# Gate loads, squares and weight sums at other points of the program, and another order at the start of the up stage and at its last pair

## The chip, the cores and the metric

The kernel runs on one NeuronCore of one Trainium2 chip. The metric is the device time of one execution in microseconds; lower is better. A core has a matrix engine (TensorE, PE in the profile, with its weight loads as PEld), three engines for elementwise work (VectorE = DVE, ScalarE = ACT, GpSimd = POOL) and SyncE (SP), which here issues most of the DMAs. The engines run their own instruction streams in order and wait for each other by semaphores.

## The reference

One layer of a hybrid encoder on a prompt of 1024 tokens and a batch of 8 x 16 sample tokens (1152 columns in the kernel). Cut to what matters here:

```python
z = rms_norm(x, g_mix) @ w_in              # latents, retention q/k/v, gates ga and gb
attn = latent_attention(z)                 # 8 heads
ret  = retention(z)                        # 4 heads, chunkwise, gated
a_d = attn @ w_o_branch[:1024]
r_d = ret  @ w_o_branch[1024:]
merged = sigmoid(ga) * a_d + sigmoid(gb) * r_d
x = x + merged @ w_out
u = rms_norm(x, g_ffn) @ w_ffn_up          # 1024 -> 2 * 2816
c = causal_conv_width_3(u) + b
x = x + (silu(c[gate]) * c[value]) @ w_ffn_down
```

The outputs are x of prompt and sample, the new latents and rope keys, the retention states and the last two rows of u.

## The kernel before

Tokens lie along the free axis (T = 1152 columns, three chunks of CH = 384), features on the 128 partitions. Every f32 factor is split into two parts, hi (a cast on ScalarE, L228) and lo (a difference on VectorE, L229), and a product is made of three matmuls, hi*hi, lo*hi and hi*lo. So before a weight tile (`wraw` loaded by SP, `whi`, `wlo`) or an activation tile can be used, ScalarE and then VectorE must have handled it.

The stages that the change touches, in order of time:

- *Gate stage* (to about 165 us). Tiles 0 to 13 of the gate weights; `gate_out` applies the sigmoid and stores the tile to `s_gate`. Between the tiles stand loads and sums for later: the up stage multiplies with sums of quarters of the up weights. `sum_load(j)` (L352, L353) has SP load the quarters `prg` and `prv`, `sum_store(j)` has POOL add them (L344 to L347, `psum`) and store them to `s_w`. Beside it runs `norm`: column sums of squares on TensorE (L339), `ss`, the power on POOL (L284, `inv`), `ivsq` (L450) and a diagonal matrix `diag` (L330) with which TensorE spreads the row over the partitions (L333). The last two sums stand in the kv stage behind it (L525).
- *Branch layers* (about 1340 to 1662 us). Three layers of 8 output tiles: `w_or` on the retention rows (`ret_out`, L1293: `xf` = product * gate), `w_oa` on the attention rows (`att_out`, L1300 and L1301: `xf` += product * gate) and `w_out` on `xf` (`res_out`). The gate tile `mg` has two buffers and is loaded by POOL's own queue. After each output tile `presum_half` lets POOL add half of a weight sum. In the third layer `mg` holds x, `res_row` adds the product (L1312), scales into `y` (L1313) and stores the sum to `s_x` (L1314); `squares` then squares `mg` in place (L1319) and adds it to `acc` (L1320).
- *Start of the up stage* (about 1662 to 1700 us). The up product splits the rows in a two-level scheme with seven blocks (b11, t1, t2, t3, t4, b21, b22), each of four row tiles k = 0 to 3. The blocks that have no place while the third layer runs are stored to memory by `combine` and come back in `reload` (tile `z`, two buffers; L1363). `last_row` handles the last output tile of the third layer, with ScalarE and VectorE held to the written order. `fourth` and `fifth` follow in `then`, which is called after each of the seven products of a pair.
- *Last pair and start of the down stage* (about 2160 to 2200 us). The convolution taps and the activation of the last pair, splits of the first down weights (`down_w`) and of the stored activations `ar`, reloaded through POOL's queue (L1565), in groups.

A scheduler places the instructions of each engine from the program order and its own costs, except inside `in_order`, where the named engines keep the written order. What stands where is read below from the instruction lists of the two built kernels.

## Time and profile before

| | us |
|---|---|
| median of 3 runs | 2457.23 (2455.23 to 2459.61) |
| the profiled execution, whole | 2458.73 |
| its span in the trace | 2456.9 |
| PE busy | 2392.1 (97%) |
| DVE busy | 1420.9 (58%) |
| ACT busy | 946.4 (39%) |
| POOL busy | 476.5 (19%) |
| mean granted clock of TensorE, of 1 | 0.983 |

The span runs from the first to the last instruction in the trace; the profiled execution took 1.83 us more. TensorE is busy nearly throughout, so time shows in two things: where it idles, and where its clock is low. In the rows of a timeline stand the start, the busy time of a run of equal instructions, engine, line, operation, output and inputs, the count, and in brackets the idle time before it with the instruction that ended it. In the waits stand the total, the count and the longest.

### The profile page before, as it was taken

How to read it: one execution, taken by the hardware profiler on the slowest of the kernel's cores; microseconds unless marked ns; L12 is line 12 of the kernel's file. 1: busy time of each engine (PE TensorE's matmuls, PEld its weight loads, DVE VectorE, ACT ScalarE, POOL GpSimd, SP SyncE). 2: the span in 40 equal slices, each digit the busy share in tenths (PEclk: the TensorE clock that was granted, in tenths of full speed). 3: DMA queues.
4: the chain of work that ended last, by engine and by line, in shares of the span. 5: the costliest groups of instructions: out<-in, count | busy, mean ns of one | idle time of the engine just before them, and what ended most of it. 6: DMA issues, size and time to landing. Idle time of an engine off the chain costs nothing.

```text
span 2456.9 us, 38559 instructions
## 1 busy us (share of the span) xinstructions
PE 2392.1 (97%) x14888; PEld 2284.6 (93%) x14888; DVE 1420.9 (58%) x2858; ACT 946.4 (39%) x2210; POOL 476.5 (19%) x727
## 2 busy tenths in 40 slices
PE   9999999999999989999999989998999999999999
PEld 8999998998999968787998989997999999999999
DVE  7233456456249857444887333557888888884442
ACT  5221333333236635664665120334333333353331
POOL 2721000000003302332110324141111111121100
PEclk9999999999999999998999989998999999999999
DMA  6952311210225576525674565373333333377652
GB/s 238 383 188 96 114 56 35 69 64 23 76 78 170 159 249 206 168 85 147 206 210 136 195 210 182 132 257 119 104 120 111 108 100 120 111 239 233 213 162 92
DMA packets 175991, 366.29 MB, mean 149 GB/s; under 512 B 15296, under 2 KB 92224, under 8 KB 174016
## 3 DMA queue, kind: packets, MB, share of 16 engines
q1 hardware_dynamic: 81728, 213.00, 26.4%
q0 software_dynamic: 35824, 88.52, 11.7%
q10 hardware_dynamic: 58256, 62.30, 7.4%
q8 instruction: 117, 1.92, 0.3%
q14 instruction: 66, 0.54, 0.1%
HBM read 252.65 MB, written 111.13 MB: 148 GB/s over the span
## 4 chain that ended last, share of the span: by engine, by line
PE 78%; DMA 6%; issue 5%; DVE 5%; POOL 4%; ACT 2%; SPq 0%; ACTq 0%; POOLq 0%; DVEq 0%
PE mm L188 48%; PE mm L1422 19%; PE sm L188 4%; DMA pr<-w_up 3%; PE sc L188 3%; PE apo L188 2%; PE apt L1140 1%; POOL psum L344 1%; DVE wlo L229 1%; POOL psum L346 1%; DMA mg<-s_gate 1%; DMA s_x<-mg 1%; POOL psum L345 1%; DMA s<-s_ret 1%; POOL psum L347 1%
## 5 line engine op out<-in xcount | busy, mean ns | idle before, releaser
L228 ACT CAST whi<-wraw 128x1024 fp32r<-128x1024 f32 (+3 forms) x223 | 221.0, 999 | 518.5 <-PE mm L188 312.3
L229 DVE TENSOR_TENSOR wlo<-wraw,whi 128x1024 fp32r<-128x1024 f32 (+3 forms) x223 | 259.1, 1168 | 199.9 <-ACT whi L228 198.6
L1422 PE MATMUL mm<-xt,whi 128*128 128x288 f32 x1408 | 284.7, 297 | 6.8 <-DVE u L1475 5.2
L1422 PEld LDWEIGHTS mm<-xt,whi 128*128 128x128 f32 x1408 | 228.4, 190 | 7.4 <-DVE u L1475 5.4
L188 PE MATMUL mm<-whi,xh 128*128 128x256 f32 (+2 forms) x720 | 228.2, 333 | 0.7 <-DVE gsig L410 0.7
L188 PE MATMUL mm<-whi,xl 128*128 128x256 f32 (+2 forms) x720 | 225.3, 329 | 0.0
L188 PE MATMUL mm<-wlo,xh 128*128 128x256 f32 (+2 forms) x720 | 224.8, 329 | 0.3 <-DVE wlo L229 0.3
L1422 PE MATMUL mm<-xb,whi 128*128 128x288 f32 x1056 | 213.0, 296 | 2.1 <-ACT r L1480 1.2
L1422 PE MATMUL mm<-xt,wlo 128*128 128x288 f32 x704 | 209.2, 297 | 0.0
L1422 PEld LDWEIGHTS mm<-xb,whi 128*128 128x128 f32 x1056 | 170.5, 189 | 2.9 <-ACT r L1480 1.4
L1422 PE MATMUL mm<-xb,wlo 128*128 128x288 f32 x528 | 156.6, 297 | 1.3 <-DVE wlo L229 1.3
L188 PE MATMUL mm<-rh,whi 128*128 128x384 f32 x576 | 135.3, 342 | 14.3 <-DVE xf L1293 8.9
L188 PEld LDWEIGHTS mm<-whi,xl 128*128 128x128 f32 x720 | 132.5, 190 | 12.1
L188 PEld LDWEIGHTS mm<-whi,xh 128*128 128x128 f32 x720 | 132.6, 190 | 10.6 <-issue 0.7
L188 PEld LDWEIGHTS mm<-wlo,xh 128*128 128x128 f32 x720 | 132.6, 190 | 9.8 <-DVE wlo L229 0.5
L188 PE MATMUL mm<-act,whi 128*128 128x384 f32 x528 | 134.3, 335 | 3.4 <-ACT whi L228 3.4
L188 PE MATMUL mm<-rl,whi 128*128 128x384 f32 x576 | 134.2, 340 | 3.4 <-DVE rl L229 3.3
L188 PE MATMUL mm<-act,dwhi 128*128 128x384 f32 x528 | 134.5, 335 | 0.0
L1422 PEld LDWEIGHTS mm<-xt,wlo 128*128 128x128 f32 x704 | 133.6, 190 | 0.0
L188 PE MATMUL mm<-rh,wlo 128*128 128x384 f32 x576 | 133.1, 338 | 0.0
L188 PE MATMUL mm<-xh,whi 128*128 128x384 f32 x528 | 123.9, 340 | 2.9 <-ACT whi L228 2.1
L188 PE MATMUL mm<-xl,whi 128*128 128x384 f32 x528 | 122.1, 337 | 0.0
(495 smaller groups left out, 5690.9 us busy)
## 6 DMA issues: line engine op xcount, KB each, us to landing
wraw<-w_dn SPq DMA_DIRECT2D x48, 512.0 KB, 3.7
s_q<-uqT ACTq DMA_DIRECT2D x36, 384.0 KB, 3.3
s_w<-psum POOLq DMA_DIRECT2D x12, 1024.0 KB, 8.7
aq<-s_q POOLq DMA_DIRECT2D x8, 1536.0 KB, 9.0
ar<-s_act POOLq DMA_DIRECT2D x21, 576.0 KB, 5.8
wraw<-w_up SPq DMA_DIRECT2D x22, 512.0 KB, 3.7
wraw<-s_w SPq DMA_DIRECT2D x22, 512.0 KB, 4.3
wraw<-s_w SPq DMA_DIRECT2D x44, 256.0 KB, 3.0
```

What stands on the lines that cost most here:

```text
L188: E.matmul(out, l, r, start=start, stop=stop)
L228: A.copy(hi, src)
L229: return V.tensor_tensor(out=lo, in0=src, in1=hi.bitcast(F32), op=ALU.subtract)
L344: G.tensor_tensor(out=s[:, 1], in0=rg[:, 0], in1=rv[:, 0], op=ALU.add)
L345: G.tensor_tensor(out=s[:, 2], in0=rv[:, 0], in1=rv[:, 1], op=ALU.add)
L346: G.tensor_tensor(out=s[:, 0], in0=s[:, 2], in1=rg[:, 0], op=ALU.add)
L347: G.tensor_tensor(out=s[:, 3], in0=s[:, 0], in1=rg[:, 1], op=ALU.add)
L1140: E.transpose(pt[:, j * 256 + e * P:j * 256 + (e + 1) * P], pm[e][:, jj * P:(jj + 1) * P], ident)
L1422: E.matmul(banks[bank][c], l[:, ks], x, start=bool(first) and k + e == 0, stop=k + e == 5, skip_group_check=not first)
```

## The change

- The sums of the gate stage: the load of a sum and its adds come one tile later; the kv stage takes three sums instead of two.
- The branch layers: the loads of the gate tiles (and of x in the third layer) come from one list, two ahead, each next one called for after a tile is used; squares of a tile are called for at the start of the next tile; t1 is made in place in `y1`.
- The start of the up stage: `reload` has three buffers; the splits of the first two weights stand ahead of the first reloads; the third weight, the last block splits, the reloads and the squares of tile 7 move among the first three products (`rest`).
- The last pair: the splits of the last third of the first down weights stand ahead of the taps of the gate half and its activation.

```diff
@@ -456,9 +456,9 @@
                 stream.start(norm())
                 for f in range(2, 13):
                     gate_out(f, fm_tile(mm, wslot(d["w_gate"][f], D), xr))
-                    if f > 2:
-                        pend.append(sum_load(f - 3, wk, 2))
                     if f > 3:
+                        pend.append(sum_load(f - 4, wk, 2))
+                    if f > 4:
                         sum_store(*pend.pop(0), wk, 2)
                 sum_store(*pend.pop(0), wk, 2)
 
@@ -522,8 +522,8 @@
                         if k == 3:
                             stream.tick()
                     stream.start(kv_out(t, ps))
-                    if t in (2, 5):
-                        pend.append(sum_load(10 + t // 5, wk, 1))
+                    if t % 3 == 1:
+                        pend.append(sum_load(9 + t // 3, wk, 1))
                     elif pend:
                         sum_store(*pend.pop(), wk, 1)
                     stream.tick()
@@ -1227,13 +1227,14 @@
-        def new_rows(mm, w, f0, f1, fill):
+        def new_rows(mm, w, f0, f1, load):
+            ahead = [load(k) for k in range(2)] if load else []
             wts = [bslot(d[w][f]) for f in (f0, f1)]
             rows = []
 
             def row(k):
                 hi, lo = slot("rh", f"r{2 * k}"), slot("rl", f"r{2 * k + 1}")
-                fill(k, hi, lo)
+                split(hi, lo, (ahead.pop(0) if ahead else load(k)) if load else xf[k])
                 rows.append((hi, lo))
                 return hi, lo
 
@@ -1256,8 +1257,8 @@
                     S.dma_start(rv, quarters(d["w_up"][NJ + j])[:, :, hs])
                 pend.append((j, hs, rg, rv))
 
-        def layer(mm, w, order, fill, out):
-            rows, first = new_rows(mm, w, order[0], order[1], fill)
+        def layer(mm, w, order, load, out):
+            rows, first = new_rows(mm, w, order[0], order[1], load)
             for i, f in enumerate(order):
                 ps = fm_tile(mm, bslot(d[w][f]), rows) if i > 1 else first[i]
                 out(f, ps)
@@ -1284,28 +1285,39 @@
 
         xf = [None] * 8
 
+        sources = [s_gate[8 + f] for f in range(8)] + [s_gate[f] for f in range(8)] + [d["x_fm"][f] for f in (0, 4, 1, 5, 2, 6, 3, 7)]
+        loaded = []
+
+        def load_g():
+            if sources:
+                g = wk.tile([P, T], F32, name="mg", bufs=2)
+                G.dma_start(g, sources.pop(0))
+                loaded.append(g)
+
+        load_g()
+        load_g()
+
         def ret_out(f, ps):
             xf[f] = slot(f"xf{f}", f"e{f}", dt=F32)
-            g = wk.tile([P, T], F32, name="mg", bufs=2)
-            G.dma_start(g, s_gate[8 + f])
+            g = loaded.pop(0)
             for c in range(NCH):
                 cs = slice(c * CH, (c + 1) * CH)
                 V.tensor_tensor(out=xf[f][:, cs], in0=ps[c], in1=g[:, cs], op=ALU.mult)
+            load_g()
 
         def att_out(f, ps):
-            g = wk.tile([P, T], F32, name="mg", bufs=2)
-            G.dma_start(g, s_gate[f])
+            g = loaded.pop(0)
             for c in range(NCH):
                 cs = slice(c * CH, (c + 1) * CH)
                 V.tensor_tensor(out=g[:, cs], in0=ps[c], in1=g[:, cs], op=ALU.mult)
                 V.tensor_tensor(out=xf[f][:, cs], in0=xf[f][:, cs], in1=g[:, cs], op=ALU.add)
+            load_g()
 
         acc = fwt.tile([P, T], F32, name="acc")
         ys = {}
 
         def res_row(f, ps):
-            g = wk.tile([P, T], F32, name="mg", bufs=2)
-            G.dma_start(g, d["x_fm"][f])
+            g = loaded.pop(0)
             y = ys[f] = wk.tile([P, T], F32, name="y", bufs=2)
             for c in range(NCH):
                 cs = slice(c * CH, (c + 1) * CH)
@@ -1321,18 +1333,27 @@
             else:
                 A.activation(acc, g, AF.Square)
 
+        unsquared = []
+
+        def settle():
+
+            if unsquared:
+                squares(*unsquared.pop())
+                load_g()
+
         ha, hb = slice(0, HT), slice(HT, T)
         late_work = []
 
         def res_out(f, ps):
             if f == 7:
                 return last_row(ps)
+            settle()
             g, y = res_row(f, ps)
             if f < 4:
                 block("b11", f, y[:, ha])
             else:
                 combine(f - 4)
-            squares(g, f)
+            unsquared.append((g, f))
 
         def combine(k):
 
@@ -1344,9 +1365,9 @@
                 else:
                     S.dma_start(s_t[name, k], src)
 
-            t1 = wk.tile([P, HT], F32, name="t1")
+            t1 = y1[:, ha]
             t2 = wk.tile([P, HT], F32, name="t2")
-            V.tensor_tensor(out=t1, in0=y1[:, ha], in1=y1[:, hb], op=ALU.subtract)
+            V.tensor_tensor(out=t1, in0=t1, in1=y1[:, hb], op=ALU.subtract)
             V.tensor_tensor(out=t2, in0=y2[:, hb], in1=t1, op=ALU.add)
             done("t2", t2)
             done("b21", y2[:, ha])
@@ -1359,20 +1380,21 @@
 
         def reload(blocks):
             for b, k in blocks:
-                z = wk.tile([P, HT], F32, name="z", bufs=2)
+                z = wk.tile([P, HT], F32, name="z", bufs=3)
                 S.dma_start(z, s_t[b, k])
                 block(b, k, z)
 
         def last_row(ps):
 
             y1 = ys[3]
-            t1 = wk.tile([P, HT], F32, name="t1")
+            t1 = y1[:, ha]
             t2 = wk.tile([P, HT], F32, name="t2")
             with in_order(ET.Activation, ET.DVE):
-                reload(late[:4])
+                settle()
                 raw = up_raw(0)
                 w = [wtile(raw[i], D, i) for i in range(2)]
-                V.tensor_tensor(out=t1, in0=y1[:, ha], in1=y1[:, hb], op=ALU.subtract)
+                reload(late[:4])
+                V.tensor_tensor(out=t1, in0=t1, in1=y1[:, hb], op=ALU.subtract)
                 block("t1", 3, t1)
                 g, y2 = res_row(7, ps)
                 V.tensor_tensor(out=t2, in0=y2[:, hb], in1=t1, op=ALU.add)
@@ -1380,25 +1402,27 @@
                 block("b21", 3, y2[:, ha])
                 V.tensor_tensor(out=y1[:, hb], in0=y1[:, hb], in1=y2[:, hb], op=ALU.subtract)
                 block("t3", 3, y1[:, hb])
-                w.append(wtile(raw[2], D, 2))
-
-            def fourth():
-                V.tensor_tensor(out=y2[:, ha], in0=y2[:, ha], in1=t2, op=ALU.subtract)
-                block("t4", 3, y2[:, ha])
-                reload(late[4:7])
-
-            def fifth():
-                block("b22", 3, y2[:, hb])
-                squares(g, 7)
-                reload(late[7:10])
-
-            late_work.extend((raw, w, fourth, fifth))
+
+            def rest(n):
+                if n == 0:
+                    w.append(wtile(raw[2], D, 2))
+                    V.tensor_tensor(out=y2[:, ha], in0=y2[:, ha], in1=t2, op=ALU.subtract)
+                    block("t4", 3, y2[:, ha])
+                    reload(late[4:5])
+                elif n == 1:
+                    reload(late[5:7])
+                    block("b22", 3, y2[:, hb])
+                else:
+                    reload(late[7:10])
+                    squares(g, 7)
+
+            late_work.extend((raw, w, rest))
 
         order = list(range(8))
         raw_row = lambda src: (lambda t: (S.dma_start(t, src), t)[1])(wk.tile([P, T], F32, name="y", bufs=2))
-        layer(mm, "w_or", order, lambda k, hi, lo: split(hi, lo, raw_row(s_ret[k])), ret_out)
-        layer(mm, "w_oa", order, lambda k, hi, lo: split(hi, lo, raw_row(s_att[k])), att_out)
-        layer(mm, "w_out", [0, 4, 1, 5, 2, 6, 3, 7], lambda k, hi, lo: split(hi, lo, xf[k]), res_out)
+        layer(mm, "w_or", order, lambda k: raw_row(s_ret[k]), ret_out)
+        layer(mm, "w_oa", order, lambda k: raw_row(s_att[k]), att_out)
+        layer(mm, "w_out", [0, 4, 1, 5, 2, 6, 3, 7], None, res_out)
 
 
 
@@ -1577,8 +1601,7 @@
         AT = [(5, 6), (7, 8), (9, 10), (13, 14), (15, 16), (19, 20), (21, 22), (23, 24)]
         AT = [tuple(DS[i] for i in t) for t in AT]
 
-        raw_w, w, fourth, fifth = late_work
-        w.append(None)
+        raw_w, w, rest = late_work
         raw_n = up_raw(1)
         prev = None
         acts, wa, wb = [], [], []
@@ -1602,14 +1625,14 @@
                         prev.tap(v, prev.uv, prev.cv, 0)
                         prev.tap(g, prev.ug, prev.cg, 1)
                     else:
-                        fourth()
+                        rest(0)
                 elif n == 1:
                     me.read_u2(ps)
                     if prev:
                         prev.tap(g, prev.ug, prev.cg, 0)
                     else:
-                        fifth()
-                    w[3] = wtile(raw_w[3], 512, 3)
+                        rest(1)
+                    w[3:] = [wtile(raw_w[3], 512, 3)]
                     if prev:
                         A.activation(prev.cg, prev.cg, AF.Silu)
                     if last:
@@ -1617,6 +1640,7 @@
                         me.rw = [down_raw(0, 0), down_raw(1, 0)]
                 elif n == 2:
                     if not j:
+                        rest(2)
                         open_up()
                     me.read_c11(ps)
                     if prev:
@@ -1700,11 +1724,11 @@
                 prev.tap(v, prev.uv, prev.cv, 0)
                 group(4)
                 group(5)
+                wa += down_w(rw[4], 2, set_a)
+                wb += down_w(rw[5], 2, set_b)
                 prev.tap(j, prev.ug, prev.cg, 1)
                 prev.tap(j, prev.ug, prev.cg, 0)
                 A.activation(prev.cg, prev.cg, AF.Silu)
-                wa += down_w(rw[4], 2, set_a)
-                wb += down_w(rw[5], 2, set_b)
                 group(6)
                 prev.product()
                 acts += act_split(prev.cv[:, None, :CH], act_tiles(AT[7]))
```

POOL's list at the end of the first branch layer and the start of the second, before: `psum` and its store are a weight sum, `s_gate14` and `15` are the gates of the last two tiles of the first layer, `s_gate0` and `1` those of the second.

```order
L347 TENSOR_TENSOR psum_16064<-psum_16064,pr_15842 128x256
L1249 DMA s_w15_142<-psum_16064 512x1x256
L1290 DMA mg_15734<-s_gate14_95 128x1152
L1290 DMA mg_15831<-s_gate15_96 128x1152
L1297 DMA mg_16056<-s_gate0_81 128x1152
L1297 DMA mg_16074<-s_gate1_82 128x1152
L344 TENSOR_TENSOR psum_16082<-pr_16070,pr_16071 128x256
```

And after:

```order
L347 TENSOR_TENSOR psum_16068<-psum_16068,pr_15846 128x256
L1250 DMA s_w15_142<-psum_16068 512x1x256
L1294 DMA mg_15547<-s_gate14_95 128x1152
L1294 DMA mg_15644<-s_gate15_96 128x1152
L1294 DMA mg_15741<-s_gate0_81 128x1152
L1294 DMA mg_15838<-s_gate1_82 128x1152
L344 TENSOR_TENSOR psum_16086<-pr_16074,pr_16075 128x256
```

Lines have other numbers; no instruction has another place here. In all three layers one of the 24 loads, the fourth, stands one sum instruction earlier.

SP's list at the start of the up stage, before: `z` are block reloads, `s_t`, `s_b` the stored blocks, `wraw` the weights of the second pair and of the rest of it, `s_x` the stores of x.

```order
L1363 DMA z_17561<-s_t320_154 128x576
L1363 DMA z_17566<-s_t100_149 128x576
L1314 DMA s_x3_114<-mg_17463 128x1152
L1363 DMA z_17571<-s_t110_150 128x576
L1363 DMA z_17576<-s_t120_151 128x576
L1363 DMA z_17670<-s_t400_155 128x576
L1363 DMA z_17675<-s_t410_156 128x576
L1212 DMA wraw_17628<-w_up 128x1024
L1212 DMA wraw_17630<-s_w1_128 128x1024
L1314 DMA s_x7_118<-mg_17602 128x1152
L1212 DMA wraw_17632<-s_w1_128 128x512
L1212 DMA wraw_17632<-w_up 128x512
```

And after:

```order
L1384 DMA z_17576<-s_t320_154 128x576
L1384 DMA z_17581<-s_t100_149 128x576
L1384 DMA z_17586<-s_t110_150 128x576
L1326 DMA s_x3_114<-mg_17354 128x1152
L1212 DMA wraw_17620<-w_up 128x1024
L1212 DMA wraw_17622<-s_w1_128 128x1024
L1384 DMA z_17591<-s_t120_151 128x576
L1384 DMA z_17666<-s_t400_155 128x576
L1384 DMA z_17700<-s_t410_156 128x576
L1384 DMA z_17705<-s_t420_157 128x576
L1326 DMA s_x7_118<-mg_17462 128x1152
L1212 DMA wraw_17624<-s_w1_128 128x512
```

The third reload moved ahead of the store of x, and the two large weight loads moved ahead of the fourth reload. On ScalarE and VectorE the splits of the first two weights now stand ahead of the splits of the first four reloads; the difference t1 and everything up to the split of t3 stays behind those four; u (L1475) stands ahead of the second and third of the next three reloads; and acc of tile 7 (L1320) behind the last three.

ScalarE's list at the last pair, before: `ar` are stored activations, `cg` the gate half, `whi` and `dwhi` the down weights.

```order
L228 CAST act_23096<-ar_22972 128x1152
L228 CAST act_23104<-ar_23011 128x1152
L228 CAST act_23108<-ar_23048 128x1152
L228 CAST act_23498<-ar_23496 128x1152
L1705 ACTIVATE cg_23082<-cg_23082 128x1168
L228 CAST whi_23115<-wraw_23042 128x768
L228 CAST dwhi_23119<-wraw_23094 128x768
L228 CAST act_23123<-ar_23100 128x1152
L228 CAST act_23504<-ar_23502 128x1152
L228 CAST act_23131<-cv_23050 128x384
```

And after:

```order
L228 CAST act_23092<-ar_22968 128x1152
L228 CAST act_23100<-ar_23007 128x1152
L228 CAST act_23104<-ar_23044 128x1152
L228 CAST whi_23108<-wraw_23038 128x768
L228 CAST dwhi_23112<-wraw_23090 128x768
L228 CAST act_23494<-ar_23492 128x1152
L228 CAST act_23500<-ar_23498 128x1152
L1731 ACTIVATE cg_23078<-cg_23078 128x1168
L228 CAST act_23119<-ar_23096 128x1152
L228 CAST act_23127<-cv_23046 128x384
```

The two weight casts moved ahead of the first reload of the second column chunk (`ar_23496` before, `ar_23492` after) and of the activation; the cast of `ar_23100` (now `ar_23096`), group 6 of the first chunk, stands behind a second reload of that chunk. TensorE's own list is the same in both kernels.

## Prediction

> **What bounds the kernel now.** I read the page's busy shares first, then the waits of TensorE, grouped by what ended them.
>
> ```profile
> span 2456.9 us, 38559 instructions
> PE 2392.1 (97%) x14888; PEld 2284.6 (93%) x14888; DVE 1420.9 (58%) x2858; ACT 946.4 (39%) x2210; POOL 476.5 (19%) x727
> ...
> PE mm L188 <- DVE xf L1293: 8.9, 1, 8.9
> ...
> PE mm L1422 <- DVE u L1475: 5.2, 1, 5.2
> ...
> PE mm L188 <- DVE mg L1300: 3.3, 2, 2.6
> ```
>
> TensorE is busy 2392.1 of 2456.9 us, so 64.8 us of idle time is all that an edit of order can win, with the clock lost behind each idle stretch. The change leaves the matmuls and their order alone. Its worth is therefore what it does to the waits above: the columns are total, number, longest. Five places are touched, and I take them one by one. The profiled execution took 2458.73 us, 1.83 more than its span and 1.5 more than the median, 2457.23; the sum goes on the former and is then set against the median.
>
> **The gate loads of the branch layers: 0.** This part ought to shorten the two largest waits it is near, 8.9 and 3.3 us. The longest one comes about like this:
>
> ```profile
> 1434.04 1.18 POOL L1290 DMA_DIRECT2D mg<-s_gate  x2
> ...
> 1439.50 1.49 DVE L1293 TENSOR_TENSOR xf<-mm,mg 128x384 f32<-128x384 f32 x3 [13.46 <-DMA mg<-s_gate]
> ...
> 1453.62 1.62 PE L188 MATMUL mm<-rh,whi 128*128 128x384 f32 x3 [8.86 <-DVE xf L1293]
> ```
>
> The gate tile is asked for at 1434.04, behind the weight sum that POOL carries (L344 to L347 and a store), lands 5.4 us later, and VectorE has idled 13.46 us for it; everything on VectorE shifts, and TensorE at last lacks a free PSUM bank. A load two tiles ahead in the program would cure that if it also stood ahead of those sums on POOL. POOL's listing in the change shows that it does not: gate 14 and 15 already stood together behind the store before the change, and stand there after it. The tile still has two buffers, so a load still waits until VectorE has read the tile two before. Over the three layers one load of 24 moves, by one sum. The squares keep their place too, except the last two. The halved difference tile (L1375 before, now in place) is free as well: ScalarE and VectorE wait for it nowhere in the waits above. Price 0, with plus or minus 1 for the one load.
>
> **The gate stage, sums a tile later: +0.9.** Its one stall is 2.91 us:
>
> ```profile
> 39.92 1.83 POOL L284 TENSOR_TENSOR inv<-ss,negh 128x9 f32<-128x9 f32 x1 [38.01 <-DVE ss L448]
> 41.73 1.28 POOL L344 TENSOR_TENSOR psum<-prg,prv 128x512 f32<-128x512 f32 x1
> ...
> 41.79 1.25 DVE L450 TENSOR_TENSOR ivsq<-inv 128x9 f32<-128x9 f32 x1 [1.95 <-POOL inv L284]
> 42.96 2.75 DVE L330 TENSOR_SCALAR diag<-ident,inv 128x128 f32<-128x128 f32 x3
> ...
> 45.77 0.91 PE L333 MATMUL sm<-diag,ones 128*128 128x384 f32 x2 [2.91 <-DVE diag L330]
> ...
> 1694.97 2.75 POOL L284 TENSOR_TENSOR i<-ss,negh 128x9 f32<-128x9 f32 x1 [43.12 <-DVE ss L1439]
> ...
> 1694.80 1.22 DVE L229 TENSOR_TENSOR wlo<-wraw,whi 128x1024 fp32r<-128x1024 f32 x1
> ...
> DMA to landing us min/median/max: 6.3/6.3/6.3
> ```
>
> VectorE's small operations from 41.79 on are stretched while POOL adds weights. If the sum came after them the stall would go. But the sum's loads move behind only one weight load: the weight load that is now ahead of them stood third before, issued at 33.95 and landing 6.3 us later (last line), at 40.2, and the sum's second operand now takes that third place. So it is there before POOL leaves the power (41.75), and the adds start right behind it as now. What does change is that wlo stands ahead of ivsq on VectorE and runs beside the power. The later power at 1694.97, with a wlo beside it, took 2.75 instead of 1.83 us. That is 0.92 more before ivsq, diag and the stalled matmul. I take +0.9; the ends are -2.9 (the sum happens to start after diag) and +3 (the second three diag, now contiguous with the first, are all held).
>
> **The start of the up stage: +5.6.** Here the order of ScalarE, VectorE and SP really changes, as SP's listing shows.
>
> ```profile
> 1662.64 0.54 PE L1422 MATMUL mm<-xb,whi 128*128 128x288 f32 x2 [0.92 <-ACT whi L228]
> 1664.43 0.43 PE L1422 MATMUL mm<-xb,wlo 128*128 128x288 f32 x1 [1.25 <-DVE wlo L229]
> ...
> 1671.54 0.40 PE L1422 MATMUL mm<-xt,whi 128*128 128x288 f32 x1 [1.21 <-ACT xt L228]
> 1672.33 0.40 PE L1422 MATMUL mm<-xt,whi 128*128 128x288 f32 x1 [0.40 <-DVE xt L229]
> ...
> 1675.67 0.54 PE L1422 MATMUL mm<-xb,whi 128*128 128x288 f32 x2 [1.21 <-ACT r L1480]
> ...
> 1684.29 0.85 PE L1422 MATMUL mm<-xt,whi 128*128 128x288 f32 x2 [5.17 <-DVE u L1475]
> ...
> 1689.48 2.06 PE L339 MATMUL sm<-ones,acc 128*128 128x1 f32 x18
> ```
>
> ```profile
> 1660.54 1.36 DVE L1320 TENSOR_TENSOR acc<-acc,mg 128x1152 f32<-128x1152 f32 x1 [4.69 <-ACT mg L1319]
> ...
> 1663.16 2.35 DVE L229 TENSOR_TENSOR wlo<-wraw,whi 128x1024 fp32r<-128x1024 f32 x2
> 1665.43 0.75 DVE L1375 TENSOR_TENSOR t<-y 128x576 f32<-128x576 f32 x1
> ...
> 1659.34 1.17 ACT L1319 ACTIVATE mg<-mg 128x1152 f32<-128x1152 f32 x1 [4.46 <-DMA s_x<-mg]
> ...
> 1674.28 1.04 ACT L228 CAST whi<-wraw 128x1024 fp32r<-128x1024 f32 x1
> 1675.23 0.69 ACT L1480 COPY r<-mm 128x288 f32<-128x288 f32 x2
> 1677.28 0.68 ACT L228 CAST xt<-y 128x576 fp32r<-128x576 f32 x1 [1.36 <-DVE y L1386]
> ```
>
> ```profile
> DMA to landing us min/median/max: 2.8/2.8/2.8
> ...
> DMA to landing us min/median/max: 4.5/4.5/4.5
> ...
> DMA to landing us min/median/max: 4.0/4.6/5.3
> ...
> 1662.60:1676.00 13.40, 9.29 (x50) 8.38 (x51) 10.00 (x14) 6.71 (x11) 0.00 (x0) 0.87 0.49 168
> ```
>
> The first two landings are those of the block reloads issued at 1662.60 and at 1655.22, the third that of the two weight loads issued at 1664.40 and 1665.54. The last line is a stretch with its length, five busy times and the granted clock, 0.87: 1.7 us of TensorE's 13.4 were lost to a clock that dropped behind waits of 2.2.
>
> The gain: wlo of the first two weights no longer follows two reloaded blocks, so it runs from 1661.9 (the end of acc) to 1664.2, and of the waits 0.92 and 1.25 some 1.4 go.
>
> The price: three reloads have buffers, the fourth needs the first one's, and the first is split only after wlo, at 1664.9. SP issues the fourth at 1665.0, right behind the two weight loads that wlo set free at 1663.1 and 1664.3. It lands after 2.8 to 4.5 us, and I take the 4.5, whose loads also stood behind a big transfer: 1669.4. VectorE and ScalarE keep the written order there, so everything behind the fourth block stands still, though TensorE itself does not need it yet. Cast 0.67 and difference 0.76 later, at 1670.7, comes the operation that stood at 1665.43. From it to the two matmuls at 1671.54 and 1672.33 were 6.1 and 6.9 us, so they come at 1676.8 and 1677.6, 5.3 later than now.
>
> From there the old waits shrink. Between 1672.33 and 1684.29 TensorE worked 5.6 us and waited 1.21 + 5.17. Now the copies of r go ahead of the third weight's cast and u ahead of two reloaded blocks. r is copied once the product ends (2.1 us of matmuls, at half clock some 3.5: 1681.1), by 1681.8; the cast takes 1.04, to 1682.8, and then come wlo (1.2 us), a difference, a cast, a difference and one block (0.7 each) before the first u (half of 0.8), 4.5 in all, so product 4 starts at about 1687.3 instead of 1684.29, and the 5.3 late have become 3.0. At full clock this product would end about 1690.5 to 1691.
>
> The last step costs again. TensorE next sums acc's columns (1689.48), and acc of tile 7 now stands behind three reloads whose buffers come free at 1686.8, 1688.3 and 1689.0: the block ahead of the two u and the two behind them. The last one lands 2.9 later, 1691.9; a cast 0.67, the square 1.17 and acc 1.36 bring 1695.1. Against 1689.48 that is +5.6. With 2.8 us for the fourth reload everything is 1.7 earlier, +3.9; with 5.3, +6.4. A lower end is -1, if the matmuls after the column sums had waited anyway.
>
> The Trainium skill, "DMA: Bandwidth & Descriptors", section "Queues, rings and completion order", says that each DMA engine consumes the descriptors of a ring in ring order. By that the fourth reload could not overtake the weight load ahead of it, issued at 1664.3 and landing 5.3 later at 1669.6; the sum would be +5.8 or more. No run shown here has a reload this close behind a weight load.
>
> **The last pair before the down stage: +1.5.**
>
> ```profile
> 2190.11 1.15 ACT L228 CAST act<-ar 128x1152 fp32r<-128x1152 f32 x1 [8.58 <-DMA ar<-s_act]
> 2191.17 1.17 ACT L1705 ACTIVATE cg<-cg 128x1168 f32<-128x1168 f32 x1
> ...
> 2194.88 1.36 DVE L229 TENSOR_TENSOR act<-ar,act 128x1152 fp32r<-128x1152 f32 x1
> ...
> 2193.11 0.61 PE L188 MATMUL mm<-act,whi 128*128 128x384 f32 x2 [3.40 <-ACT whi L228]
> ...
> 2197.33 0.51 PE L188 MATMUL mm<-act,whi 128*128 128x384 f32 x2
> ...
> DMA to landing us min/median/max: 4.3/4.6/5.5
> ```
>
> ScalarE idles 8.58 us for an activation reload while the weight's cast stands behind it. The cast moves ahead, and the wait of 3.40 vanishes. But TensorE then needs, two steps of 1.04 us on (at 2191.8), the split group 6, which in ScalarE's listing now stands behind two reloads and the activation: 2191.2 for the first, 2193.4 for the second (issued at 2186.7; the three reloads of that group took 4.3 to 5.5 us, so it lands by 2192.2), 2194.5 the activation, 2195.6 its cast and 2197.0 its difference. TensorE goes on at about 2197.0 with the step that stood at 2197.33 before: -0.4. But the wait of 5.2 us comes behind the two steps instead of ahead of them, and so does the clock that it throws down, at some 2 us, as the 1.7 above. Sum +1.5, between -3.4 (the reloads land early) and +3.
>
> **Sum.** 0 + 0.9 + 5.6 + 1.5 = +8.0, so 2466.7 for the profiled execution and 2465.2 against the median, 0.3% slower.
>
> **The rivals.**
> - *The early weights win.* Were the fourth block in place by 1662.9, VectorE would not be held: 1.4 of the first waits, the 1.21, and the 5.17 would go with 3 us of clock, and the last pair's 3.4 might come too: 11 to 14 us, 2443 to 2446; half of it gives 2450. For it speaks the third buffer, against it that the fourth reload can't be issued before 1664.9. 0.15.
> - *The gate loads do come earlier.* 8.9 + 3.3 us and half a dozen of clock: about 2440. The order on POOL speaks against it. 0.08.
> - *The moves cancel.* Every move only trades one wait of a chain for another on the same chain, since the reloads were limited by SP before as well; the idle time stays, 2453 to 2462. For it: TensorE's order is untouched and the two largest waits stay. 0.29.
> - *More is lost.* The gate stage at +3 and the pair at +3 with +6.4: 2470. It is part of the forecast's upper end.
>
> **How the numbers follow.** The forecast, 2462 to 2472, has 0.48. About 0.2%, 4.9 us, is what a measurement of this kernel tells from no change. Faster by more: 0.15 + 0.08 and a little of the third, 0.25; within: 0.27; slower: 0.48. The range leaves out the gate loads' 2440 and the best of the first rival: 2446 to 2471.
>
> **What would show it.** The wait of 8.9 at the end of the first branch layer stays. The first weights' waits shrink to under 1 us; then a new wait of 6 to 8 us for xt stands where 1.21 did, u's is under 3, and the column sums wait 3 to 5 us for acc. At 2189 no wait for whi, and one of 4 to 6 us for act two steps on. I am wrong if TensorE passes the column sums earlier than before, or if the gate tile's load stands ahead of the sums' landing.

## The result and the profile after

The changed kernel takes 2483.61 us (median of 4 runs, 2483.03 to 2485.66), the one before 2456.64 beside it (4 runs, 2455.23 to 2459.61): a ratio of 1.011, with an interval of 1.0092 to 1.0127. It is 27 us slower. The forecast was 2465.2 with a range up to 2471, so the sign was right and the size was not.

The head of the page and the waits of TensorE after the change (total, number, longest):

```profile
span 2483.8 us, 38569 instructions
...
PE 2393.0 (96%) x14888; PEld 2285.6 (92%) x14888; DVE 1424.9 (57%) x2858; ACT 946.8 (38%) x2210; POOL 478.9 (19%) x727
```

```profile
PE mm L188 <- ACT whi L228: 12.6, 3, 8.4
PE mm L1446 <- ACT xt L228: 11.2, 1, 11.2
PE mm L188 <- DVE xf L1305: 7.9, 1, 7.9
...
PE mm L188 <- ACT act L228: 6.3, 1, 6.3
PE mm L188 <- ACT rh L228: 6.1, 1, 6.1
PE sm L339 <- DVE acc L1332: 4.9, 1, 4.9
...
PE sm L333 <- DVE diag L330: 4.0, 2, 3.8
```

TensorE's busy time is the same to 0.9 us (2392.1 before); what grew is its idle time, from 64.8 to 90.8 us. Three waits were forecast in kind (xt, longer than the 6 to 8 us expected, act and acc). Two were not: one of 8.4, listed under whi, and rh with 6.1 instead of 2.1, which run 8 takes up. Both kernels run the same 14888 matmuls in the same order, so each one of after can be set against the same one of before. How far after is behind, by the starts of the matmuls, then shows where the time goes:

| stretch (time in the trace before) | lag ahead of it | lag behind it | added | forecast |
|---|---|---|---|---|
| first 30 us | 0 | 2.1 | +2.1 | none |
| gate stage, 45 to 60 | 2.1 | 3.5 | +1.4 | +0.9 |
| start of the kv stage, 181 to 184 | 3.5 | 13.2 | +9.7 | no term |
| 184 to 1335 | 13.2 | 12.9 | -0.3 | 0 |
| branch layers, 1336 to 1530 | 12.9 | 13.7 | +0.8 | 0 |
| start of the up stage, 1662 to 1702 | 13.7 | 22.4 | +8.7 | +5.6 |
| last pair, 2193 to 2203 | 22.4 | 26.9 | +4.5 | +1.5 |

The first row comes from a first wait for weights, 2.77 us instead of 0.82, with the same instructions ahead of it; in the kernels of the experiments, which are equal there, this lag is anything from nothing to over 3 us in single profiles. I don't count it to the change. The others are read one by one.

**The kv stage.** After the change, SP and POOL (the waiting load and what it waits for), ScalarE, VectorE and TensorE, from a timeline of each (start, busy time, instruction, idle time before it and what ended it), and then the landing of the first `w_rg` load:

```profile
178.89 0.33 SPq L352 DMA_DIRECT2D prg<-w_up  x1
...
179.79 0.97 SPq L288 DMA_DIRECT2D wraw<-w_rg  x2
...
177.57 1.29 POOL L347 TENSOR_TENSOR psum<-psum,prg 128x512 f32<-128x512 f32 x1
...
188.76 1.04 ACT L228 CAST whi<-wraw 128x1024 fp32r<-128x1024 f32 x1 [13.53 <-DMA wraw<-w_rg]
...
191.33 1.15 ACT L228 CAST whi<-wraw 128x1152 fp32r<-128x1152 f32 x1 [0.45 <-ACT gsig L411]
...
189.84 2.07 DVE L229 TENSOR_TENSOR wlo<-wraw,whi 128x1024 fp32r<-128x1024 f32 x1 [9.77 <-ACT whi L228]
191.83 1.47 DVE L410 TENSOR_TENSOR gsig<-mm,ivb 128x384 f32<-128x384 f32 x3
...
192.52 0.82 PE L188 MATMUL mm<-whi,xh 128*128 128x288 f32 x2 [8.44 <-ACT whi L228]
```

```profile
DMA to landing us min/median/max: 9.0/9.0/9.0
```

The same place in the kernel before:

```profile
171.89 7.26 SPq L288 DMA_DIRECT2D wraw<-w_rg  x2
...
180.10 1.15 ACT L228 CAST whi<-wraw 128x1152 fp32r<-128x1152 f32 x1 [1.64 <-PE mm L188]
...
180.98 0.50 PE L188 MATMUL mm<-whi,xh 128*128 128x288 f32 x2 [0.39 <-DVE gsig L410]
```

```profile
DMA to landing us min/median/max: 3.4/3.4/3.4
```

Read it from the bottom. The kv stage's first matmul waits for two engines, and the profile names the one that ended last, the cast at 191.33. But that cast is not what it needs: in the kernel before, the same matmul starts at 180.98, ahead of the end of the cast (180.10 + 1.15). It needs the PSUM bank, TensorE's output memory, from which VectorE still has to read the last gate product (`gsig`). In all 14 profiles it starts 0.14 or 0.15 us after the first of the three gsig operations has ended, in the kernel after at 192.37; that the cast ends in the same 0.2 us is chance. The gsig operations stand on VectorE behind the difference of `w_rg` (189.84), which waits for its cast (188.76), and ScalarE has idled 13.53 us for that load. SP issued it at 179.79 instead of from 171.89 on, because the loads of one more weight sum stand ahead of it. Those need the buffer `prg`, of which the kv stage has one, and which POOL reads until 178.86 (177.57 + 1.29). The issue is only part of the delay. Less the 3.5 us that this kernel was already behind, `w_rg` goes out 4.4 us later, and then it takes 9.0 us to land instead of 3.4: the two loads of the sum and POOL's store of another one are issued within the 0.9 us ahead of it. So a load that nobody needs soon holds up another one on SP and goes ahead of it, that one's split on ScalarE and VectorE holds up the reading of the gate product, and TensorE stands 8.44 us, with 1.6 more behind it at a lower clock (0.58 of full speed from 192 to 197 us).

**The start of the up stage.** After the change, TensorE, SP and ScalarE, and then, from the view of its transfers, the landing of the fourth reload:

```profile
1675.99 0.53 PE L1446 MATMUL mm<-xb,whi 128*128 128x288 f32 x2 [0.56 <-ACT whi L228]
...
1693.11 0.61 PE L1446 MATMUL mm<-xt,whi 128*128 128x288 f32 x1 [11.16 <-ACT xt L228]
...
1702.00 0.54 PE L1446 MATMUL mm<-xt,whi 128*128 128x288 f32 x2 [0.94 <-DVE u L1499]
...
1710.32 4.00 PE L339 MATMUL sm<-ones,acc 128*128 128x1 f32 x18 [4.86 <-DVE acc L1332]
...
1678.69 0.32 SPq L1212 DMA_DIRECT2D wraw<-s_w  x1
1679.36 8.08 SPq L1384 DMA_DIRECT2D z<-s_t  x4
...
1685.63 0.67 ACT L228 CAST xt<-z 128x576 fp32r<-128x576 f32 x1 [7.03 <-DMA z<-s_t]
```

```profile
DMA to landing us min/median/max: 6.2/6.2/6.2
```

This is the forecast chain, longer: the fourth reload is issued at 1679.36, right behind a weight load, takes 6.2 us, and everything behind its cast on ScalarE and VectorE stands still. The xt wait, the short u wait and the acc wait follow in the forecast order. The column sums then take 4.00 us instead of 2.06.

**The last pair.** After the change, ScalarE, SP and TensorE, and then the landing of the second activation reload, issued at 2209.15:

```profile
2212.35 1.16 ACT L228 CAST act<-ar 128x1152 fp32r<-128x1152 f32 x1 [6.92 <-DMA ar<-s_act]
2217.23 1.15 ACT L228 CAST act<-ar 128x1152 fp32r<-128x1152 f32 x1 [3.71 <-DMA ar<-s_act]
2218.28 1.17 ACT L1731 ACTIVATE cg<-cg 128x1168 f32<-128x1168 f32 x1
...
2209.74 1.20 SPq L1212 DMA_DIRECT2D wraw<-w_dn  x2
...
2220.55 0.69 PE L188 MATMUL mm<-act,whi 128*128 128x384 f32 x1 [6.32 <-ACT act L228]
```

```profile
DMA to landing us min/median/max: 8.0/8.0/8.0
```

The weight's cast is early, its wait of 3.40 is gone, and the wait for act has come behind it, as forecast. The second reload took 8.0 us, with two weight loads issued 0.6 and 1.5 us after it.

### The profile page after: what moved, and what is told of

Same layout as the page of the kernel before. It is cut to its first block, busy times and chain, and to the rows that moved or that the text cites. A ratio compares the mean times of both kernels' runs of the same rounds, so it can differ in the third digit from the quotient of the medians.

```text
span 2483.8 us, 38569 instructions
## 1 busy us (share of the span) xinstructions
PE 2393.0 (96%) x14888; PEld 2285.6 (92%) x14888; DVE 1424.9 (57%) x2858; ACT 946.8 (38%) x2210; POOL 478.9 (19%) x727
## 4 chain that ended last, share of the span: by engine, by line
PE 74%; DMA 9%; DVE 6%; issue 4%; POOL 4%; ACT 3%; SPq 1%; ACTq 0%; POOLq 0%; DVEq 0%
PE mm L188 44%; PE mm L1446 19%; PE sm L188 4%; DMA pr<-w_up 3%; PE sc L188 3%; PE apo L188 2%; PE apt L1140 1%; DMA s<-s_ret 1%; DVE wlo L229 1%; DMA s_x<-mg 1%; DMA y<-s_ret 1%; POOL psum L347 1%; POOL psum L346 1%; POOL psum L344 1%; POOL psum L345 1%
## 5 line engine op out<-in xcount | busy, mean ns | idle before, releaser
L188 PEld LDWEIGHTS mm<-rh,whi 128*128 128x128 f32 x576 | 104.7, 191 | 20.6 <-DVE xf L1305 8.6
```

The costliest lines, as they stand in the source:

```text
L188: E.matmul(out, l, r, start=start, stop=stop)
```

## The experiments

All but the last three stand on the kernel after the change with one thing altered (6 adds to 5, and 9 to 3). "Local" is the difference of the matmuls' lag across the place in question, in the profiled executions, one for each kernel, and stretches that no edit touches differ between them by up to 4 us or so; the ratio is that of the times to the kernel before, measured beside it.

**1. The tenth sum back in the gate stage.** Theory Q: the 9.7 us of the kv stage are the third sum's loads ahead of `w_rg` on SP. The sums stay a tile late, but the tenth is added at the gate stage's end, with two buffers, and two are left for the kv stage.

```diff
+                pend.append(sum_load(9, wk, 2))
+                sum_store(*pend.pop(0), wk, 2)
                 sum_store(*pend.pop(0), wk, 2)
...
-                    if t % 3 == 1:
-                        pend.append(sum_load(9 + t // 3, wk, 1))
+                    if t in (2, 5):
+                        pend.append(sum_load(10 + t // 5, wk, 1))
```

> The changed kernel with the tenth sum loaded and added at the end of the gate stage again, so that the kv stage has two sums as before; the other sums stay a tile later. Theory Q (SP's queue holds the third kv sum's loads for a free buffer, the w_rg weights wait behind them, their cast on ScalarE waits, and the cast of the last kv weights stands behind that one): the wait of 8.4 us for whi at the start of the kv stage goes, and 9 to 10 us of the 27 with it, so 2473 to 2475; the 1.3 us in the gate stage stay. Rival W (the kv stage starts late because everything in the gate stage comes a tile later and more bytes are under way): the wait stays at 6 us or more and the time within 2 us of 2483.6.

Measured: 2472.14 us (2469.43 to 2477.86), ratio 1.0066 (1.0045 to 1.0086). SP in this kernel:

```profile
166.24 0.38 SPq L288 DMA_DIRECT2D wraw<-w_gate  x1
177.19 7.25 SPq L288 DMA_DIRECT2D wraw<-w_rg  x2
```

The loads of `w_rg` are directly behind the gate weights again, the wait of 8.44 at the kv stage is 0.39, and locally 9.7 us are won. The first `w_rg` load lands in 3.4 us again. Theory Q holds but for its last link, which is gsig and not the cast of the last kv weights: a single sum at another place is over a third of the loss.

**2. The sums on time, three in the kv stage.** The complement of 1.

```diff
-                    if f > 3:
-                        pend.append(sum_load(f - 4, wk, 2))
-                    if f > 4:
+                    if 2 < f < 12:
+                        pend.append(sum_load(f - 3, wk, 2))
+                    if 3 < f < 12:
                         sum_store(*pend.pop(0), wk, 2)
```

> The opposite part alone: the gate stage's sums on time as before, but the tenth sum still in the kv stage, three there. Theory Q: the 8.4 us wait at the kv stage stays, only the 1.3 us of the gate stage go, so 2481 to 2484. Rival W: the wait goes with the late sums, 2473 to 2475.

Measured: 2480.03 us (2478.6 to 2481.48), ratio 1.0095 (1.0079 to 1.011). TensorE at the gate stage's stall:

```profile
49.27 0.91 PE L333 MATMUL sm<-diag,ones 128*128 128x384 f32 x2 [2.91 <-DVE diag L330]
```

The gate stage's stall is 2.91 as before the change (3.80 with the sums late), and the kv stage's wait stays, at 8.2. The two are independent: the delay of the sums costs 0.9 in the stall, the third kv sum the rest. All five profiles with the sums on time have 2.9 there, the nine with the sums late 3.8.

**3. The start of the up stage as before** (two reload buffers, reloads ahead of the first weights, the old `fourth` and `fifth`), with the branch layers as after.

```diff
                 settle()
+                reload(late[:4])
                 raw = up_raw(0)
                 w = [wtile(raw[i], D, i) for i in range(2)]
-                reload(late[:4])
...
+                w.append(wtile(raw[2], D, 2))
...
-                    reload(late[4:5])
+                    reload(late[4:7])
...
-                    reload(late[5:7])
                     block("b22", 3, y2[:, hb])
-                else:
-                    reload(late[7:10])
                     squares(g, 7)
+                    reload(late[7:10])
```

> The changed kernel with the start of the up stage as before (two reload buffers, four reloads ahead of the first weights, t1 in place kept). Theory: the waits of 11.2 (xt) and 4.9 (acc) go and those of before come back, 0.9, 1.3, 1.2, 1.2 and 5.2; net -8.6 us, 2474 to 2476. Rival (the up stage starts late because of the branch layers, and the reloads are slow because of that): less than 4 us gained.

Measured: 2477.2 us (2474.32 to 2479.43), ratio 1.0079 (1.0061 to 1.0098); locally 3.9 us are won, not 8.7, and 4.8 of the loss stay. Of the waits of TensorE:

```profile
PE mm L1444 <- DVE u L1497: 6.0, 2, 5.8
...
PE mm L1444 <- ACT whi L228: 5.6, 1, 5.6
```

The waits for xt (1.22 again) and acc are gone as expected, and u's 5.8 is back. But the first up weights now keep TensorE waiting 5.6 us, where the kernel before had 0.92. So the branch part has a price that shows only with the old order. Runs 9 and 10 ask where it is from.

**4. The last pair as before.**

```diff
-                wa += down_w(rw[4], 2, set_a)
-                wb += down_w(rw[5], 2, set_b)
                 prev.tap(j, prev.ug, prev.cg, 1)
                 prev.tap(j, prev.ug, prev.cg, 0)
                 A.activation(prev.cg, prev.cg, AF.Silu)
+                wa += down_w(rw[4], 2, set_a)
+                wb += down_w(rw[5], 2, set_b)
                 group(6)
```

> The changed kernel with the last pair's order as before. Theory: the waits of 6.3 and 0.7 for act go, 3.4 for whi comes back; net -4.4 us, 2478 to 2480. Rival (the lost time is a shift of the down stage's transfers that the order does not set): within 1.5 us of 2483.6.

Measured: 2480.75 us (2475.45 to 2485.17), ratio 1.0097 (1.0073 to 1.012). The wait for whi is back with 3.32, those for act are gone, and locally 4.3 us are won. The last pair's part of the loss is this one move.

**5. The fourth reload later.** Theory Z: the xt wait is the fourth reload, which has no buffer yet, in the written order.

```diff
-                reload(late[:4])
+                reload(late[:3])
...
-                    reload(late[4:5])
+                    reload(late[3:5])
```

> The changed kernel with only three reloads ahead of t1; the fourth (t1 of row tile 2, which TensorE needs only in the fifth product) comes after the split of t4. Theory Z (the fourth reload, standing behind two weight loads on SP, holds ScalarE and VectorE in their written order): the wait of 11.2 us for xt falls to 4 to 6, the 4.9 for acc stays, and the time falls by 5 to 7 us to 2476 to 2479. Rival B (the reloads are late because the transfers are full, so whichever comes next is late): the wait moves to the next reload and less than 2 us are gained.

Measured: 2476.92 us (2476.69 to 2477.27), ratio 1.0082 (1.0067 to 1.0097). Of the waits of TensorE:

```profile
PE sm L339 <- DVE acc L1332: 5.9, 1, 5.9
...
PE mm L1446 <- ACT xt L228: 4.7, 1, 4.7
```

xt's wait falls from 11.16 to 4.7, and the acc wait grows by one, from 4.9 to 5.9: locally 5.6 us are won. Theory Z holds.

**6. Besides, the squares ahead of the last reloads.** Run 5 with the squares of tile 7 called for at the start of the second `rest` instead of at the end of the third.

```diff
                 elif n == 1:
+                    squares(g, 7)
                     reload(late[5:7])
                     block("b22", 3, y2[:, hb])
                 else:
                     reload(late[7:10])
-                    squares(g, 7)
```

> The same, and the squares of tile 7 ahead of the last six reloads instead of behind them. Theory Z: the 4.9 us for acc at the column sums go as well, 10 to 12 us in all, 2472 to 2474. Rival B: TensorE waits as long for another operand behind the column sums, and nothing is gained over the run with the fourth reload late.

Measured: 2470.72 us (2465.93 to 2475.81), ratio 1.0057 (1.0039 to 1.0075). The acc wait is gone, xt keeps 4.7, u has 1.8 at most, and locally some 10.6 us are won, 1.9 more than the whole loss at this place. So acc was late because it stood behind the last reloads, not because the square itself or the sums before it took longer.

**7. Group 6 ahead of the taps and the activation.** Theory G: the act wait of the last pair is group 6 standing behind the gate half's activation; its rival: the wait only moves.

```diff
                 wb += down_w(rw[5], 2, set_b)
+                group(6)
                 prev.tap(j, prev.ug, prev.cg, 1)
                 prev.tap(j, prev.ug, prev.cg, 0)
                 A.activation(prev.cg, prev.cg, AF.Silu)
-                group(6)
```

> The changed kernel with the split of group 6 right behind the last weight splits, ahead of the taps and the activation. Theory G (the two reloads of the next chunk and the activation stand ahead of group 6 on ScalarE, and the second of those reloads is late because the w_dn loads now go beside it): the waits of 6.3 and 0.7 for act go with 3 us of clock, 8 to 10 us, 2474 to 2476. Rival: the product of the pair, now behind group 6, comes later and TensorE waits for it instead; less than 4 us.

Measured: 2478.3 us (2474.37 to 2479.74), ratio 1.0089 (1.0073 to 1.0106). ScalarE and TensorE:

```profile
2208.83 1.15 ACT L228 CAST act<-ar 128x1152 fp32r<-128x1152 f32 x1 [3.10 <-DMA ar<-s_act]
2209.89 1.17 ACT L1732 ACTIVATE cg<-cg 128x1168 f32<-128x1168 f32 x1
...
2212.92 1.28 PE L188 MATMUL mm<-act,whi 128*128 128x384 f32 x2 [4.38 <-ACT act L228]
```

Group 6 is in time, but the activation still stands behind the casts of the two other reloads, of which the second took 8.4 us to land (the cast of the first line), and TensorE waits 4.38 us for the split of the product that the activation feeds. Locally only 2.5 us are won. The theory holds for the place of the wait, the rival for its worth: whoever comes last of two reloads and an activation on ScalarE is waited for.

**8. The y tiles made ahead of the first gate tiles.** Theory M: the branch layers' longer first wait (rh, 6.10 instead of 2.06) comes from the places in memory. The tile pool gives the first gate tiles, now made earlier, a place that the y tiles had. Here the first two y tiles are made first; the instructions and their order on TensorE stay.

```diff
-        load_g()
-        load_g()
-
...
             ahead = [load(k) for k in range(2)] if load else []
+            if w == "w_or":
+                load_g()
+                load_g()
```

> The changed kernel with the first two y tiles taken from the pool ahead of the first two gate tiles, as before, so that they lie where they lay; no instruction has another place. Theory M (the change of places in memory made the first y loads wait for the last attention tiles): they are issued some 10 us earlier again, the first wait of 6.1 us for rh falls to 2 to 3, and behind the stall at the end of the first layer 0 to 1.5 us of it are left, 2482 to 2484. Rival (the y loads are late for their place on SP): the 6.1 stay.

Measured: 2484.18 us (2479.99 to 2488.18), ratio 1.0111 (1.0096 to 1.0127). The y loads and the first product, in the kernel after and then in this one:

```profile
1347.75 9.04 SPq L1422 DMA_DIRECT2D y<-s_ret  x3
1353.77 1.65 PE L188 MATMUL mm<-rh,whi 128*128 128x384 f32 x4 [6.10 <-ACT rh L228]
```

```profile
1334.59 16.97 SPq L1422 DMA_DIRECT2D y<-s_ret  x4
1346.36 1.54 PE L188 MATMUL mm<-rh,whi 128*128 128x384 f32 x4 [2.06 <-ACT rh L228]
```

And what SP's queue waited for ahead of these loads, again first in the kernel after and then in this one:

```profile
SPq L1422 <- PE apo L188: 30.2, 1, 30.2
```

```profile
SPq L1422 <- PE sc L188: 32.5, 1, 32.5
```

In the kernel after, the first y load waits for other matmuls of the attention (apo instead of sc) and goes out 13 us later, of which the kernel after was 3 us behind already; with the y tiles first, the old wait of 2.06 is back. Theory M holds for the wait. By the third layer it is worth 0.5 us in these two profiles, too little to be seen in the time.

**9. The up stage as before and the squares outside the written order.** Theory S: the 5.6 us of run 3 come from `settle`, which stands inside `in_order` there. The edit is that of run 3 and this one:

```diff
             with in_order(ET.Activation, ET.DVE):
-                settle()
                 reload(late[:4])
```

with `settle()` on the line ahead of the block.

> As the run with the start of the up stage as before, but with the squares of the tile ahead called for outside the written order of ScalarE and VectorE, as before. Theory S (in that earlier run the square, which waits for the store of x, stood in the written order ahead of the reloads and cost the 5 us at the first up product): the wait of 5.6 us for whi falls to 1 to 2 and the whole gain of 8.6 us appears, 2473 to 2476. Rival: the 5.6 us have another cause (transfers) and stay, 2477 to 2480.

Measured: 2479.02 us (2477.87 to 2481.26), ratio 1.0087 (1.0061 to 1.0113). The wait for the first up weights stays, at 6.2, as the rival said, though not for its reason. The instruction list of ScalarE is the same as in run 3, with the square ahead of the first two reloads' casts; in the kernel before, two casts stood ahead of it. So theory S falls where it blames the written order, and the place of the square, which this edit did not move, is not tested by it.

**10. The branch part alone.** Gate loads, later squares and t1 in place; sums, up stage and last pair as before. The edits are those of run 9, run 4 and the old sums.

> Only the part on the branch layers (gate tiles and y rows ahead, squares at the next tile, t1 in place); gate and kv stage, up stage and last pair as before. Forecast on record for this part: 0, plus or minus 1. Theory M: the first wait for rh is 6 instead of 2 us, the wait at the end of the first layer 8 instead of 8.9, 0 to 2 us in all, 2457 to 2460. Rival (the parts help each other: alone this one brings its gate tiles early): the wait of 8.9 falls below 6 and the time below 2454.

Measured: 2462.71 us (10 runs, 2457.92 to 2469.06) beside 2456.43 (23 runs), ratio 1.0028 (1.0013 to 1.0043). This is above the 2457 to 2460 of theory M, and the rival's wait below 6 did not come (it is 7.4). ScalarE and TensorE at the start of the up stage:

```profile
1653.20 1.17 ACT L1331 ACTIVATE mg<-mg 128x1152 f32<-128x1152 f32 x1 [5.82 <-DMA s_x<-mg]
1654.27 1.24 ACT L228 CAST xt<-z 128x576 fp32r<-128x576 f32 x2
...
1659.39 1.29 ACT L228 CAST xt<-z 128x576 fp32r<-128x576 f32 x2 [3.88 <-DMA z<-s_t]
...
1661.68 0.85 PE L1444 MATMUL mm<-xb,whi 128*128 128x288 f32 x2 [5.70 <-ACT whi L228]
```

The square waits 5.82 us for the store of x (it squares in place), and the first reloads' casts stand behind it. They free the two buffers, so reloads 3 and 4 come later (ScalarE idles 3.88 for them), and the first up weights' cast is behind these. Through the three layers this kernel loses 0.3 us, at the up start 4.2. By the trace this chain is the 5.6 of run 3, which has it too; no run puts the square alone back behind the casts. In the kernel after, the weights are cast ahead of the reloads, and this price is hidden: its whi wait is 0.56.

**11. An order from these results.** Sums as before, y tiles first, last pair as before; at the up start the weights first, then only blocks of tiles in place; a reload is called for where its buffer is free, and the squares of tile 7 stand ahead of the first one:

```diff
                 raw = up_raw(0)
                 w = [wtile(raw[i], D, i) for i in range(2)]
-                reload(late[:4])
                 V.tensor_tensor(out=t1, in0=t1, in1=y1[:, hb], op=ALU.subtract)
-                block("t1", 3, t1)
...
+                    w.append(wtile(raw[2], D, 2))
+                    squares(g, 7)
+                    reload(late[:1])
+                elif n == 1:
+                    block("t1", 3, t1)
+                    reload(late[1:4])
...
```

> An attempt to beat both: gate, kv and last pair as before, y tiles ahead of gate tiles in memory, and at the start of the up stage the weights first, then only what TensorE needs next: t2, b21, t3, then the third weight, acc of tile 7 and the one t3 reload, u, and after it t1, t4 and b22. Theory (the order of VectorE's work, not its amount, sets the stalls there): the waits of 11.2 and 4.9 fall below 2.5 together, 4 to 9 us less than before, 2449 to 2454. Rival (VectorE is full between the first up weights and u3, so a wait only moves to the sixth or seventh product): within 2.5 us of before.

Measured: 2453.95 us (12 runs, 2449.52 to 2462.45) beside 2456.43 (23 runs), ratio 0.9995 (0.9981 to 1.0009): no difference that these runs can tell. TensorE:

```profile
1688.18 0.82 PE L1446 MATMUL mm<-xt,whi 128*128 128x288 f32 x2 [8.81 <-DVE u L1499]
```

TensorE runs 17.0 us ahead of the kernel before by the end of the first products, with a lead of 5.9 at the end of the branch layers. Then it stands 8.81 us for a u that is behind all block splits on VectorE, and leaves with a lead of 6.3, little more than it came with. The waits that left the first products all stand ahead of one later product, as the rival had it.

**12. The up stage of run 6 alone.** Sums and last pair as before, y tiles first, and the up start of run 6.

> The weight sums and the last pair as before, the y tiles made ahead of the first gate tiles, and the up start of the changed kernel with the fourth reload later and the squares of tile 7 ahead of the last reloads (run z_and_squares_early). Theory (the parts add up): the up start alone is some 2.8 us better than before in the profile, the branch layers within 1.5 of before, nothing lost elsewhere, so 2452 to 2455 beside 2456.5, a ratio of 0.998 to 1.000; the xt wait stays at 4.7, no acc wait, u under 2. Rival (the gain is eaten behind it): the up start's lag has come back to 0 within 30 us behind the column sums, by a wait for u or whi of 3 us or more, and the ratio is 1.000 to 1.002.

Measured: 2452.46 us (11 runs, 2451.08 to 2458.05) beside 2456.26 (15 runs), ratio 0.9992 (0.9982 to 1.0002). Of the waits of TensorE:

```profile
PE mm L1446 <- ACT xt L228: 4.7, 1, 4.7
```

There is none for acc, and those for u are 1.9 at most. In the profile the lead grows from 5.6 to 8.0 us over the up start and is 6.8 at the end, so 2.4 are won there and not given back within 30 us; 1.2 go again at the last pair. The up start behaves as theory had it. But a gain of one in a thousand is within the interval's reach of no change: no version here is shown to beat the kernel before.

## Why the prediction was wrong

**The step that failed** is in "The gate stage, sums a tile later: +0.9". It followed the moved sums through the gate stage alone. The third sum that the edit puts into the kv stage was known (the change says "three sums instead of two") and got no price, neither for its adds nor for its two loads on SP. These loads stand ahead of `w_rg`, wait there for the one buffer, lengthen its landing from 3.4 to 9.0 us, and cost 9.7 us, the largest single part (runs 1 and 2). How much of it is the wait for the buffer and how much the order alone was not tried apart. Both could be seen ahead of the run: SP's list has the loads in this order, and in the profile before POOL still adds the sum ahead of them until 174.37, 2.5 us after `w_rg` had gone out. The "more is lost" rival added up the upper ends of terms already in the sum and could not hold it.

**The gate stage itself** was right, mechanism included. The power took 2.75 us instead of 1.83, with a wlo beside it on VectorE:

```profile
42.01 2.75 POOL L284 TENSOR_TENSOR inv<-ss,negh 128x9 f32<-128x9 f32 x1 [40.11 <-DVE ss L448]
```

The stall went from 2.91 to 3.80, as the +0.9 said; up to 60 us it is 1.4.

**The branch layers, 0.** Right: the stall for xf stays (7.92 after 8.86), as the order on POOL had said. Two things were missed that cost little here: earlier gate tiles move the y tiles in memory (run 8), and the squares do not "keep their place". A square called for one tile later stands ahead of the first reloads' casts, and costs some 4 us where these are cast ahead of the weights (run 10). That the change hides it is luck of the combination: alone, this part makes the kernel slower, by a ratio of 1.0028.

**The start of the up stage, +5.6** was right as a mechanism and too small. The fourth reload came behind the two weight loads as forecast, but took 6.2 us, not the chosen 4.5. The weight load ahead of it, issued at 1678.69, landed at 1684.9, the reload at 1685.6, 0.7 later. That is how the rule of the Trainium skill ("DMA: Bandwidth & Descriptors", "Queues, rings and completion order") would have it, with the descriptors of a ring consumed in ring order; the same section says that a later transfer may still finish its write ahead of an earlier one, so the rule alone does not settle it, and the trace does. TensorE took up xt 7.9 later than before (forecast 5.3), was 4.0 behind at the start of the product that waits for u (3.0), and 7.1 at the column sums (5.6). The remaining 1.6 of the 8.7 are the clock behind that wait, which the sum had left out here and counted at the last pair:

```profile
1708.00:1725.00 17.00, 14.69 (x75) 13.62 (x76) 9.65 (x22) 4.51 (x8) 3.03 (x3) 0.70 0.29 87
```

The granted clock (third from the end) is 0.70 in the 17 us around the column sums. Moving the fourth reload back cut the wait for xt from 11.16 to 4.7, and moving the squares forward took the one for acc away (runs 5 and 6), so both steps are the right ones.

**The last pair, +1.5.** The wait moved from whi to act two steps on, as forecast, but the second reload, said to take at most 5.5 us, took 8.0, with two weight loads issued right behind it, and the group's split came 2.4 later than thought. The forecast also stopped at group 6: run 7 shows that with the group in time the product's split is waited for, 4.4 us.

Of the 26.9 us by which the profile is later, 8.0 were forecast, 9.7 had no term, 3.1 and 3.0 are the up start and the last pair beyond their terms (two landings taken too short, and the clock behind them), 2.1 are the first wait of this execution, and 1.0 the gate stage beyond its term, the branch layers and the stretch ahead of them. In the range, nothing stood for a part of the edit without a term.

## What to carry to other kernels

When a load is put into a queue, look at what it waits for and at what stands behind it on the same queue; then follow that load's first user on its engine and see what stands behind that one. Count the landing of a load from that of the loads ahead of it, not from its own issue. A load that nobody needs, with a buffer that isn't free, held TensorE here through two engines that had nothing to do with it. And when every engine near a place keeps a written order and is nearly full, an instruction that is put early makes the next one late: count the work up to the last consumer of the stretch, not up to the first.

## What the runs showed of the hardware

A reload of 128 x 576 f32, issued 0.7 us behind a weight load on the same queue, landed in 6.2 us, where such reloads had taken 2.8 to 4.5 in the kernel before. All nine profiles that have such a pair agree: the reload took 5.4 to 6.3 us and landed 0.7 to 0.8 us after the weight load. A weight load ahead is not the only thing that makes a reload long: in the profile after, the third reload, issued at 1665.66 with no weight load close ahead of it, took 6.3 us too, and why stays open. The `w_rg` load took 9.0 us with the two loads of a sum issued within 0.9 us ahead of it, and 3.4 without them (before and run 1).

The second activation reload on POOL's queue took 7.1 to 8.4 us in the nine profiles in which two weight loads were issued on SP 0.6 and 1.5 us after it, and 5.5 to 5.7 in the five with the last pair as before, where none came within 7 us. Run 4 differs from the kernel after in this order alone, with 5.6 instead of 8.0.

Stalls of 5 to 8 us were each followed by 1.6 to 2.4 us more lag at a low clock (the kv stage 1.6 at 0.58 from 192 to 197 us, the column sums 1.6 at 0.70 from 1708 to 1725, the last pair 2.4 at 0.56 from 2220 to 2228). One wait that no edit touched, for th near 900 us, was 6.1 to 6.7 us in the profiles of before, after and run 12 and 2.8 to 3.6 in those of the other runs; why stays open.
